# A hybrid two-layer backbone on one core: a weight split ahead of the mLSTM rows, layer 0's last two product blocks together, and keys, values and queries in 512 columns

## The chip, the cores and the metric

The kernel runs on 1 core of one Trainium2 chip. A core has TensorE (PE, matrix products), VectorE (DVE), ScalarE (ACT), GpSimd (POOL) and SyncE (SP, which issues most DMAs). Each engine works through its own instructions in a fixed order and waits at semaphores for the others. The metric is the device time of one execution in microseconds (us).

## The reference, cut to what matters

The inputs are 512 latent tokens `x` and 256 context tokens `ctx`, 1024 wide, a conditioning vector, and the weights of two layers. All arithmetic is float32. Only the latent stream is the output.

```python
for l in range(2):
    h_lat, h_ctx = modulate(x, ...), modulate(ctx, ...)      # RMSNorm * (1+scale) + shift
    if l == 0:  y_ctx, y_lat = mixer_ab(...)   # h @ w_in -> HGRN2 heads and mLSTM heads -> @ w_out
    else:       y_ctx, y_lat = mixer_c(...)    # attention, 8 query heads, 2 key/value heads
    x = x + g1 * rmsnorm(y_lat, norm_g[l, 1])
    x = x + g2 * rmsnorm(swiglu(modulate(x, ...), ffn_w_in[l], ffn_w_out[l]), norm_g[l, 3])
    if l == 0: the same two lines for ctx

def swiglu(h, w_in, w_out):                    # d_ff = 2816
    g, u = split(h @ w_in); return (silu(g) * u) @ w_out

def mixer_c(h_ctx, h_lat, w_qkv, qk_g, w_out, ang, need_ctx):    # the last layer needs no y_ctx
    q, k, v = split(h @ w_qkv, [1024, 1280])   # 8, 2 and 2 heads of 128
    q, k = rmsnorm(q, qk_g[0]), rmsnorm(k, qk_g[1])              # over the 128 of a head
    latent tokens: q, k = rope2d(q, ang), rope2d(k, ang)
    return softmax(q @ k_all.T) @ v_all @ w_out

mLSTM gates, per head and direction (running over tokens, reset at the start):
    m_t = max(logf_t + m_{t-1}, i_t);  b_t = sum of logf in the chunk;  weights exp(i - b), exp(-m), ...
```

## The kernel before, in words

**Products.** Every float32 operand of a product is split into a high part (rounded on ACT) and a low part (the difference, on DVE), and a product is three matmuls: high by high, high by low, low by high. `wsplit` loads a weight piece of 128 x 1024 (`raw`) by a DMA on SP's queue, makes `wh` on ACT (L128) and `wl` on DVE (L129), and keeps both instructions in `self.split`. `w_main`, `w_ext` and `w_more` do this from three rings of buffers. `proj_t` (L163) makes columns of features, `proj_n` (L181) rows of tokens: for a pair of token tiles and 256 weight columns, 2 tiles x 8 depths x 3 = 48 matmuls. Results stand in PSUM: two buffers `psa` of 1024 columns, three `psb` of 512, one `psc`.

**Order.** A scheduler puts the program's operations on each engine's queue; its order is not that of the source everywhere, but follows it. `self.after(n, fn)` queues a piece of work until `deferred()` has been called n times: by this the vector work behind a product, and the transposes of its result, are put behind later products. `behind(cx, insts)` holds what is written in its block back until the given instructions have been issued.

**Layer 0.** The HGRN2 heads are scanned one after another; while a head is scanned, a generator (`dense`) issues the next products. For the last head this is `mlstm_first`: the gates, the row operations over all tokens (`mlstm_rows`, scans on DVE, L924 to L955), the values (`v_group`, L181), then the query and key chunks `mlstm_qk(0)` and `(2)`, each with a weight of 128 columns (2560 and 2816) through L163. The scan of the last HGRN2 head uses L718 (transposes), L728 (state updates into `psb`), L733 and L735 (DVE, which read that `psb`) and L745 (scores into `psb`).

**Layer 0's second FFN product** (`ffn0_out`, L1528) goes over two halves of three token tiles and 11 blocks of 256 features. In each block each of the three tiles gets 12 matmuls of 512 columns; after the last block each tile is finished by `end`: residual and norm (`residual`: ACT L194 sums squares, DVE L188 adds the epsilon, POOL L189 takes the power, DVE L1135 and L1142), a second norm (L194, L188, L189, L1153), and, for a pair of tiles, transposes on PE (L388), scale and shift on ACT (L395) and the split into `hh`, `hl` on DVE (L402, L403), which are the moving operand of layer 1. The third tile of a half is summed in two `psb` and copied out first (L1492).

**Layer 1's projections** (`mixer1`): keys of a pair of tiles, values of that pair, three pairs; then queries of two heads at a time (256 columns) for the two latent pairs. A unit's result is squared (L1657) and copied (L1660) on ACT, summed (L1662), scaled (L1665 or L1669), rotated (L1683, L1686, L1687) on DVE, transposed on PE (L1695) and split (L1698, L1699). Values are split at L1722, L1723. Scores are L1773, the row maximum L1776, the exponential L1779, the transposes of probabilities L1789, the sums with values L1802. The output projection is `mixer1_out` (L1226), then comes the FFN of layer 1, whose first products (L163, `early`) run for two runs of 256 tokens each. The last token tile is finished by half rows (L1238 to L1246).

The constants that the change touches are:

```python
L1D = 2
L1E = 3
A1 = (3, 3, 2)
```

## Time and profile before

| | us |
|---|---|
| median of 3 runs (1667.42 to 1667.67) | 1667.49 |
| profiled execution | 1672.43 |
| its span | 1670.7 |
| PE busy in the span | 1616.4 (97%) |
| DVE busy | 1094.4 (66%) |
| ACT busy | 677.9 (41%) |
| POOL busy | 140.4 (8%) |

The mean granted clock of TensorE over the span was 0.989. Times in the profile are microseconds from the span's start. A timeline row gives start, duration, engine, line of the kernel, operation, output <- inputs and, in brackets, how long the engine stood idle before and for whom. Matmuls are pipelined, so their durations overlap. Line numbers are those of the kernel before; in the changed kernel they are 2 to some 25 higher.

### The profile page before, as it was taken

How to read it: one execution, taken by the hardware profiler on the slowest of the kernel's cores; microseconds unless marked ns; L12 is line 12 of the kernel's file. 1: busy time of each engine (PE TensorE's matmuls, PEld its weight loads, DVE VectorE, ACT ScalarE, POOL GpSimd, SP SyncE). 2: the span in 40 equal slices, each digit the busy share in tenths (PEclk: the TensorE clock that was granted, in tenths of full speed). 3: DMA queues.
4: the chain of work that ended last, by engine and by line, in shares of the span. 5: the costliest groups of instructions: out<-in, count | busy, mean ns of one | idle time of the engine just before them, and what ended most of it. 6: DMA issues, size and time to landing. Idle time of an engine off the chain costs nothing. (4 is left out here: it accounts for less than half of the span.)

```text
span 1670.7 us, 25343 instructions
## 1 busy us (share of the span) xinstructions
PE 1616.4 (97%) x10257; PEld 1427.5 (85%) x10257; DVE 1094.4 (66%) x1718; ACT 677.9 (41%) x1026; POOL 140.4 (8%) x222
## 2 busy tenths in 40 slices
PE   7999989999999999999999999899999999999997
PEld 4888878889888999999988888898898888888885
DVE  5797996655446989898856674677765533343444
ACT  4565653435335333333334453435663432222221
POOL 2000010001000001000010010212220000000001
PEclk9999999999999999999999999899999999999998
DMA  9333102223624554454439875230004623333321
GB/s 331 94 115 89 27 14 64 77 90 94 209 79 125 178 156 134 142 181 130 157 137 321 313 263 170 96 106 21 26 30 139 204 83 101 101 101 101 91 74 50
DMA packets 172289, 209.38 MB, mean 125 GB/s; under 512 B 7952, under 2 KB 143212, under 8 KB 172172
## 3 DMA queue, kind: packets, MB, share of 16 engines
q1 hardware_dynamic: 167676, 194.85, 36.7%
q0 software_dynamic: 4208, 12.59, 2.1%
q8 instruction: 80, 1.31, 0.3%
q14 instruction: 37, 0.30, 0.1%
q10 hardware_dynamic: 288, 0.33, 0.1%
HBM read 189.62 MB, written 18.12 MB: 124 GB/s over the span
## 5 line engine op out<-in xcount | busy, mean ns | idle before, releaser
L129 DVE TENSOR_TENSOR wl<-raw,wh 128x1024 fp32r<-128x1024 f32 x166 | 201.9, 1222 | 220.1 <-ACT wh L128 219.1
L128 ACT CAST wh<-raw 128x1024 fp32r<-128x1024 f32 x166 | 174.0, 1053 | 395.9 <-PE psa L163 122.7
L181 PE MATMUL psa<-wh,hh 128*128 128x256 f32 x608 | 175.3, 288 | 0.8 <-DVE qn L1669 0.7
L181 PE MATMUL psa<-wl,hh 128*128 128x256 f32 x608 | 173.7, 286 | 0.0
L181 PE MATMUL psa<-wh,hl 128*128 128x256 f32 x608 | 173.4, 285 | 0.0
L163 PE MATMUL psa<-h1h,wh 128*128 128x512 f32 (+1 forms) x384 | 142.8, 372 | 0.0
L163 PE MATMUL psa<-h1l,wh 128*128 128x512 f32 (+1 forms) x384 | 142.7, 372 | 0.0
L163 PE MATMUL psa<-h1h,wl 128*128 128x512 f32 (+1 forms) x384 | 142.6, 371 | 0.0
L181 PEld LDWEIGHTS psa<-wh,hh 128*128 128x128 f32 x608 | 117.5, 193 | 5.0 <-issue 3.5
L181 PEld LDWEIGHTS psa<-wl,hh 128*128 128x128 f32 x608 | 117.6, 193 | 0.8 <-issue 0.8
L181 PEld LDWEIGHTS psa<-wh,hl 128*128 128x128 f32 x608 | 117.6, 193 | 0.3 <-issue 0.2
L189 POOL TENSOR_TENSOR r<-e,mhalf 128x1 f32<-128x1 f32 (+2 forms) x61 | 51.0, 837 | 673.4 <-DVE e L188 673.3
L1528 PE MATMUL psa<-wh,gh 128*128 128x512 f32 x352 | 100.9, 396 | 2.6 <-ACT gh L1476 2.0
L1340 PE MATMUL psa<-hh,wX 128*128 128x384 f32 x320 | 89.8, 339 | 1.3 <-DVE ed L1360 1.3
L163 PEld LDWEIGHTS psa<-h1l,wh 128*128 128x128 f32 x384 | 72.3, 188 | 12.5
L163 PEld LDWEIGHTS psa<-h1h,wh 128*128 128x128 f32 x384 | 72.3, 188 | 12.4
L163 PEld LDWEIGHTS psa<-h1h,wl 128*128 128x128 f32 x384 | 72.3, 188 | 12.4
L1528 PEld LDWEIGHTS psa<-wh,gh 128*128 128x128 f32 x352 | 65.8, 190 | 18.8 <-ACT gh L1476 3.2
L311 DVE SCALAR_TENSOR_TENSOR oall<-oall,sil 128x1024 f32<-128x1024 f32 x50 | 62.3, 1278 | 2.4 <-DMA oall<-in_ada_w_dram 2.3
L1340 PEld LDWEIGHTS psa<-hh,wX 128*128 128x128 f32 x320 | 58.5, 188 | 4.4 <-DVE ed L1360 2.0
L163 PE MATMUL psa<-hh,wl 128*128 128x256 f32 x208 | 54.9, 343 | 5.8 <-DVE wl L129 5.8
L163 PE MATMUL psa<-hh,wh 128*128 128x256 f32 x208 | 55.4, 344 | 0.0
(454 smaller groups left out, 3848.7 us busy)
## 6 DMA issues: line engine op xcount, KB each, us to landing
raw<-in_ffn_w_in_dram SPq DMA_DIRECT2D x68, 512.0 KB, 3.8
raw<-in_ffn_w_out_dram SPq DMA_DIRECT2D x66, 512.0 KB, 4.2
adaw<-in_ada_w_dram SPq DMA_DIRECT2D x46, 512.0 KB, 4.5
oall<-in_ada_w_dram SPq DMA_DIRECT2D x34, 512.0 KB, 4.5
raw<-in_ab_w_in_dram SPq DMA_DIRECT2D x32, 512.0 KB, 4.1
rawu<-in_ffn_w_in_dram SPq DMA_DIRECT2D x20, 512.0 KB, 4.5
gd<-g POOLq DMA_DIRECT2D x22, 384.0 KB, 3.8
gr<-gd SPq DMA_DIRECT2D x22, 384.0 KB, 4.6
```

The costliest lines, as they stand in the source:

```text
L128: self.split = [nc.scalar.copy(hi, raw).ins, nc.vector.tensor_tensor(lo, raw, hi.bitcast(F32), ALU.subtract).ins]
L129: nc.vector.tensor_tensor(lo, raw, hi.bitcast(F32), ALU.subtract).ins]
L163: mm(ps[:, o:o + n], st[:, k, :], mv[:, k, t0:t0 + n], start=first, stop=last)
L181: mm(o, a[:, k, t0:t0 + P], b[:, k % 4, :], start=k == 0 and j == 0, stop=k == KD - 1 and j == 2)
L189: self.powered = nc.gpsimd.tensor_tensor(r, e, self.mhalf[:, :n], ALU.pow).ins
L311: nc.vector.scalar_tensor_tensor(av, wv, self.sil[:, k, v:v + 1], av, ALU.mult, ALU.add)
L1340: mm(dst, s[:, k, :], v[:, k, :], start=first and k == 0 and j == 0, stop=k == 3 and j == 2, skip_group_check=True)
L1528: mm(ys[ti][hf], st, mv[:, 0, hf * 512:(hf + 1) * 512], start=b == 0 and j == 0 and st is ah and mi == 0, stop=b == NF // 2 - 1 and j == 1 ...
```

## The change

Five edits:

1. `mlstm_first` issues the first step of the values and loads and splits the weight of columns 2560 first; the row operations are held behind the DVE half of that split (`self.split[1:]`).
2. In `ffn0_out` the last two blocks of a half are worked as one group: each token tile gets the four weight chunks, 24 matmuls of 512 columns, in one go, and is finished after them. `A1` goes from (3, 3, 2) to (3, 2, 2).
3. In `mixer1` keys and values are one product of 512 columns (`key_values`), and so are the queries of heads 0 to 3; heads 4, 5 and 6, 7 keep 256 columns. The weight pieces are then 2 depths x 512 columns, four of them. The ring of extra buffers grows from 4 to 6; the transposes of keys and of heads 0 to 3 are put off by one `deferred()`, those of heads 6, 7 by four (`L1E`).
4. The first products of layer 1's FFN move into `ffn_early`, whose first half runs ahead of the last deferred work of `mixer1_out`.
5. For the last tile, the epsilon's addition (`eps_added`, line L188) is what the deferred work of the tile before is held behind, in place of the addition of the two partial sums.

The core of the diff:

```diff
-L1E = 3
+L1E = 4
-A1 = (3, 3, 2)
+A1 = (3, 2, 2)
...
     def proj_n(self, ws, hT, pair):
...
+        m, n = ws[0][0].shape[1:]
         for t in range(2):
-            o = ps[:, t * 512:t * 512 + 256]
+            o = ps[:, t * 512:t * 512 + n]
...
-        self.mlstm_rows()
-            run(v_group(3072, 0, self.vb, 129))
+            values = v_group(3072, 0, self.vb, 129)
+            next(values)
+            ws = self.chunk_w(2560)
+            with ExitStack() as cx:
+                self.behind(cx, self.split[1:])
+                self.mlstm_rows()
+            run(values)
             yield
-            for b in (0, 2):
-                self.qk[b] = self.mlstm_qk(b)
+            self.qk[0] = self.mlstm_qk(0, ws)
+            self.qk[2] = self.mlstm_qk(2)
...
-        self.added = [nc.vector.tensor_tensor(ms[:, 0:1], ms[:, 0:1], ms[:, 1:2], ALU.add).ins]
+        nc.vector.tensor_tensor(ms[:, 0:1], ms[:, 0:1], ms[:, 1:2], ALU.add)
         r = self.rstd(ms[:, 0:1], 1)
+        self.added = [self.eps_added]
...
+            group = range(n, n + 2 if b == NF // 2 - 2 else n + 1)
+            for m in group:
+                if m + 2 < len(blocks):
+                    prep(m + 2)
+                self.steps(bg, 1 + half)
...
+            ops = [(*ready[m][0:2], ready[m][2], j) for m in group for j in range(2)]
...
-                if b == NF // 2 - 1:
+                if len(ops) == 4:
                     end(3 * half + ti, tiles[ti])
...
+    def ffn_early(self, l, hT):
+
+        early = {c: list(self.halves(l, c)) for c in (0, 1)}
+        for d in range(2):
+            for c in early:
+                for w, ps in early[c]:
+                    self.proj_t(ps, *w, *hT, segs=((256 * d, 256 * d, 256),))
+            self.deferred()
+            yield
+        self.early = {c: [ps for _, ps in x] for c, x in early.items()}
...
+            def unit(c0, pair, later=1):
                 ps = self.proj_n(ws[c0], hT, pair)
...
                 self.deferred()
+                for n in range(0, ps.shape[2], 256):
+                    queries(c0 + n, ps[:, :, n:n + 256], pair, later)
+
+            def key_values(pair):
+                ps = self.proj_n(ws[1024], hT, pair)
+                self.deferred()
+                kn = self.qk_norm(ps[:, :, 0:256], tp, False)
...
+                self.after(1, lambda: self.to_t(kn, kh, kl, 0, pair * 256))
...
+                for pair in range(3):
+                    key_values(pair)
...
+                ws[0] = self.natural_w(w2, 0, (self.w_ext,) * 3 + (self.w_main,), 512)
+                for pair in (1, 2):
+                    unit(0, pair)
+                ws[512] = self.natural_w(w2, 512)
+                for pair in (1, 2):
+                    unit(512, pair, L1D)
+            ws[768] = self.natural_w(w2, 768, (self.w_more, self.w_main))
+            rest = [1, 2]
+            self.attend(qh, ql, kh, kl, vh, vl, lambda: unit(768, rest.pop(0), L1E) if rest else None)
...
-        self.deferred(2)
+        self.deferred()
...
+                early = self.ffn_early(1, (hh, hl))
+                next(early)
+            for _ in early:
+                pass
```

What the schedule makes of it, at three places. In the rows below a name's last number counts the buffers of a program; the two programs number them apart.

DVE at the mLSTM rows, before: `wl_2933` is the low part of the weight of columns 2560, `wl_3008` that of 2816; L955 is the last of the row operations, L733 and L735 belong to the HGRN2 scan.

```order
L951 COPY bt_2670<-z_2514 32x6
L952 COPY bt_2670<-z_2514 32x6
L955 TENSOR_TENSOR cf_2680<-ig_2512,z_2514 64x768
L129 TENSOR_TENSOR wl_2933<-raw_2930,wh_2932 128x1024
L129 TENSOR_TENSOR wl_3008<-raw_3005,wh_3007 128x1024
L974 TENSOR_TENSOR m_2650<-z_2514,m_2650 64x768
L733 COPY st_2863<-psb_2864 128x128
```

The same place now, first ahead of the rows (L934 is the first scan) and then behind them (L738 and L740 are the old L733 and L735):

```order
L692 TENSOR_TENSOR suf_2629<-dec_2621 128x6
L129 TENSOR_TENSOR wl_2720<-raw_2717,wh_2719 128x1024
L693 TENSOR_TENSOR pre_2628<-pre_2628,dec_2621 128x6
L694 TENSOR_TENSOR suf_2629<-suf_2629,dec_2621 128x6
L934 SCALAR_TENSOR_TENSOR m_2723<-lf_2516,ig_2512 32x768
```

```order
L961 COPY bt_2743<-z_2514 32x6
L962 COPY bt_2743<-z_2514 32x6
L965 TENSOR_TENSOR cf_2753<-ig_2512,z_2514 64x768
L129 TENSOR_TENSOR wl_3008<-raw_3005,wh_3007 128x1024
L738 COPY st_2869<-psb_2870 128x128
```

One of the two splits moved ahead of the scans, the other did not; L974 moved behind the scan's steps.

DVE at the end of layer 0, before: `x_1500_10002` is the last token tile, L1153 writes its normalised rows, which PE transposes; the L402/L403 are those of the pair of tiles before.

```order
L1135 TENSOR_TENSOR x_1500_10002<-x_1500_10002,G_9266 128x1024
L1662 TENSOR_REDUCE msq_10115<-qsq_10113 128x4
L402 CAST hh_8545<-mod_10129 128x2x256
L188 TENSOR_SCALAR e_10117<-msq_10115 128x4
L403 TENSOR_TENSOR hl_8546<-mod_10129,hh_8545 128x2x256
L402 CAST hh_8545<-mod_10139 128x2x256
L402 CAST hh_8545<-mod_10149 128x2x256
L403 TENSOR_TENSOR hl_8546<-mod_10139,hh_8545 128x2x256
L403 TENSOR_TENSOR hl_8546<-mod_10149,hh_8545 128x2x256
L402 CAST hh_8545<-mod_10159 128x2x256
L403 TENSOR_TENSOR hl_8546<-mod_10159,hh_8545 128x2x256
L1142 SCALAR_TENSOR_TENSOR x_1500_10002<-x_1500_10002,r_10009,res_10000 128x1024
```

And now (L404, L405 are the old L402, L403; L1145, L1152 and L1163 the old L1135, L1142 and L1153; `x_1508_10042` is the last tile):

```order
L404 CAST hh_8545<-mod_10018 128x2x256
L405 TENSOR_TENSOR hl_8546<-mod_10018,hh_8545 128x2x256
L404 CAST hh_8545<-mod_10028 128x2x256
L405 TENSOR_TENSOR hl_8546<-mod_10028,hh_8545 128x2x256
L190 TENSOR_SCALAR e_10048<-ms_10046 128x1
L1145 TENSOR_TENSOR x_1508_10042<-x_1508_10042,G_9266 128x1024
L1152 SCALAR_TENSOR_TENSOR x_1508_10042<-x_1508_10042,r_10049,res_10040 128x1024
L190 TENSOR_SCALAR e_10106<-ms_10104 128x1
L1163 TENSOR_SCALAR res_10040<-x_1508_10042,r_10107 128x1024
```

The four pairs of L402/L403 stand ahead of the whole chain of the last tile instead of in its middle; on PE they belong to transposes that now follow the last L1528 at once.

DVE behind the second unit of 512 query columns, now (`ql` is the low part of transposed queries, whose `psb` PE has just written; `qn_10562` and `qn_10580` are the two halves of the unit, `msq_10675` belongs to the unit of 256 that follows; L1679, L1682, L1700, L1703, L1704 and L1716 are the old L1662, L1665, L1683, L1686, L1687 and L1699):

```order
L129 TENSOR_TENSOR wl_10766<-raw_10763,wh_10765 128x1024
L1716 TENSOR_TENSOR ql<-psb_10546,qh 128x2x256
L1716 TENSOR_TENSOR ql<-psb_10553,qh 128x2x256
L1679 TENSOR_REDUCE msq_10564<-qsq_10560 128x4
L190 TENSOR_SCALAR e_10566<-msq_10564 128x4
L1682 TENSOR_TENSOR qn_10562<-qn_10562,r_10567 128x512
L1700 TENSOR_TENSOR rot_10571<-qn_10562,sg_10220 128x4x32 x4
L1679 TENSOR_REDUCE msq_10582<-qsq_10578 128x4
L1703 TENSOR_TENSOR qn_10562<-qn_10562,cg_10219 128x512
L190 TENSOR_SCALAR e_10584<-msq_10582 128x4
L1704 TENSOR_TENSOR qn_10562<-qn_10562,rot_10571 128x512
```

PE's transposes of these two halves (L1712, the old L1695) stand 10 and 39 products of 256 columns into the unit after the next, with one whole narrow unit ahead of them; before, each such transpose had one or two whole narrow units ahead of it:

```order
L183 MATMUL psa_10689<-wh_10598,hh_8545 128x256
L1712 MATMUL psb_10657<-ident,qn_10562 128x128 x4
L183 MATMUL psa_10689<-wl_10599,hh_8545 128x256
L183 MATMUL psa_10689<-wh_10598,hl_8546 128x256
L183 MATMUL psa_10689<-wh_10604,hh_8545 128x256
```

The number of matmuls falls by 240 (those of L181 from 1824 to 1584); the numbers of DVE, ACT, POOL and DMA instructions stay.

More of the change, by code (lines that the diff above doesn't have):

```diff
@@ L1509, in ffn0_out @@
         prep(1)
-        for n, (half, b) in enumerate(blocks):
+        n = 0
+        while n < len(blocks):
+            half, b = blocks[n]
             if b == 0:
@@ L1514, in ffn0_out @@
                 tiles.append(ys[2])
-            if n + 2 < len(blocks):
-                prep(n + 2)
-            self.steps(bg, 1 + half)
+            group = range(n, n + 2 if b == NF // 2 - 2 else n + 1)
[3 more added lines that the diff above has]
+                self.steps(bg, 1 + half)
             if half and b < 4:
                 self.deferred()
-            gh, gl, w = ready.pop(n)
+            ops = [(*ready[m][0:2], ready[m][2], j) for m in group for j in range(2)]
+            n = group[-1] + 1
             for ti in range(3):
-                for j in range(2):
+                for q, (gh, gl, w, j) in enumerate(ops):
                     s = slice(ti * P, (ti + 1) * P)
@@ L1533, in ffn0_out, with halves @@
                     pieces.pop(0)()
+    def halves(self, l, c):
+        both = self.psa()
+        for n in range(2):
+            w = (self.w_more if (c, n) == (1, 1) else self.w_main)(self.cols(self.i["ffn_w_in"][l], n * DFF + c * P), KD, P)
+            yield w, both[:, n * 512:(n + 1) * 512]
+    def ffn_early(self, l, hT):
[7 more added lines that the diff above has]
+        self.early = {c: [ps for _, ps in x] for c, x in early.items()}
     def ffn(self, l, hT, tiles, pool, emit, yacc, bg=iter(())):
@@ L1550, in ffn @@
             c += nb
-        def half_w(c, n):
-            return (self.w_more if (c, n) == (1, 1) else self.w_main)(self.cols(win, n * DFF + c * P), KD, P)
-        def halves(c):
-            both = self.psa() if lat_only else None
-            for n in range(2):
-                yield ahead.pop((c, n), None) or half_w(c, n), both[:, n * 512:(n + 1) * 512] if lat_only else self.psa()
-        ahead = {(c, n): half_w(c, n) for c in range(2) for n in range(2)}
         def products(bi, gt, wo):
@@ L1592, in ffn @@
         G = None
[L1594 to L1601 removed]
+        early = self.early
         for bi, blk in enumerate(blocks):
@@ L1609, in ffn @@
                     pg = []
-                    for n, (w, ps) in enumerate(halves(c)):
+                    for w, ps in self.halves(l, c):
                         self.proj_t(ps, *w, *hT, segs=segs)
@@ L1853, in mixer1_out @@
                                                              c0=(i // 2 - 1) * 256))
-        self.deferred(2)
+        self.deferred()
     def run(self):
```

76 lines of the change are left out of this document (27 added, 49 removed).

## The prediction

> **What bounds the kernel now.** I read the page first, then the waits of TensorE (PE), then the timeline around each long wait.
>
> ```profile
> PE 1616.4 (97%) x10257; PEld 1427.5 (85%) x10257; DVE 1094.4 (66%) x1718; ACT 677.9 (41%) x1026; POOL 140.4 (8%) x222
> ...
> PE psa L163 <- DVE wl L129: 5.8, 1, 5.8
> PE psb L388 <- DVE res L1153: 4.1, 3, 2.7
> PE psb L1695 <- DVE qn L1687: 2.4, 1, 2.4
> PE psa L1773 <- ACT pr L1779: 2.3, 2, 1.9
> PE psa L1528 <- ACT gh L1476: 2.0, 1, 2.0
> ```
>
> PE is busy for 97% of the span, so a change can win in two ways only: fewer or shorter PE steps, and shorter stops of PE. The second group of rows (us in total, times, longest) names the stops in the places that are edited. What a matmul costs is not its listed duration, since matmuls overlap; it is the distance between two starts:
>
> ```profile
> 1300.29 0.28 PE L163 MATMUL psa<-h1h,wl 128*128 128x256 f32 x1
> 1300.41 0.28 PE L163 MATMUL psa<-h1h,wh 128*128 128x256 f32 x1
> ...
> 1274.75 0.62 PE L1226 MATMUL psa<-wh,ql 128*128 128x512 f32 x2
> 1275.20 0.62 PE L1226 MATMUL psa<-wh,qh 128*128 128x512 f32 x2
> ```
>
> 256 columns take 0.120 us (48 of L181 take 5.76), 512 columns 0.226 (two in 0.453). A stop costs more than itself when the granted clock drops after it:
>
> ```profile
> 1057.00:1080.00 23.00, 18.77 (x123) 17.64 (x122) 17.74 (x37) 12.17 (x25) 4.95 (x5) 0.78 0.29 98
> ...
> 1146.80:1150.20 3.40, 1.61 (x9) 0.96 (x7) 3.40 (x10) 1.95 (x5) 0.91 (x1) 1.00 0.00 0
> 1150.20:1153.60 3.40, 2.93 (x11) 2.74 (x12) 2.53 (x6) 0.59 (x3) 0.91 (x1) 0.50 0.00 0
> ```
>
> The columns after the length are busy times of PE, weight loads, VectorE (DVE), ScalarE (ACT), GpSimd (POOL), then the clock. After 3.4 us in which PE worked only 1.61, the next 3.4 us ran at 0.50, worth up to 1.7 us of work.
>
> The sum below is made against the profiled execution, 1672.43 us (span 1670.7, 1.7 around it), which is 4.9 above the median of runs, 1667.49; differences are carried over to the median unchanged.
>
> **The change, part by part**
>
> *1. Split ahead of the mLSTM rows.*
>
> ```profile
> 249.04 0.95 DVE L955 TENSOR_TENSOR cf<-ig,z 64x768 f32<-64x768 f32 x1
> 249.91 2.35 DVE L129 TENSOR_TENSOR wl<-raw,wh 128x1024 fp32r<-128x1024 f32 x2
> 254.15 0.29 DVE L733 COPY st<-psb 128x128 f32<-128x128 f32 x1 [1.02 <-PE psb L728]
> 255.51 0.35 DVE L735 SCALAR_TENSOR_TENSOR st<-st,dt,psb 128x128 f32<-128x128 f32 x1
> ...
> 256.84 0.30 PE L745 MATMUL psb<-qe,sp 128*32 128x64 f32 x7
> ```
>
> PE now stands 5.8 us for the first of two splits, which DVE does only after the row scans. In the new order that split runs before the scans, so this wait goes. But the next thing is late then: the second group of L745 writes a PSUM buffer whose last reader is L735, and L735 still stands behind the scans and the other split. The rows now end one split (1.15) later, at 251.1; then the other split to 252.2, L733 to 252.5, two L735 (0.35 each, one start 0.38 after the other) to about 253.3, PE at 253.4 instead of 256.84: 3.4 earlier. Four of L163 that stood ahead are still to be done (0.7), and the half clock after the stop now falls on the work behind it (about 0.7 more). Gain **2.0**; bounds 1.0 (the stop keeps its length) and 3.4.
>
> *2. Last two blocks of layer 0's second product together, and the normalising of its last tile.*
>
> ```profile
> 1051.04 0.62 PE L1528 MATMUL psb<-wh,gh 128*128 128x512 f32 x2
> 1057.25 1.47 PE L388 MATMUL psb<-ident,res 128*128 128x128 f32 x12
> 1068.93 3.19 PE L388 MATMUL psb<-ident,res 128*128 128x128 f32 x13 [2.75 <-DVE res L1153]
> ...
> 1059.03 1.22 DVE L1135 TENSOR_TENSOR x<-x,G 128x1024 f32<-128x1024 f32 x1
> 1064.76 1.28 DVE L1142 SCALAR_TENSOR_TENSOR x<-x,r,res 128x1024 f32<-128x1024 f32 x1
> 1068.12 0.75 DVE L1153 TENSOR_SCALAR res<-x,r 128x1024 f32<-128x1024 f32 x1 [0.72 <-POOL r L189]
> ```
>
> The product ends at T = 1051.5. The chain of its last tile (L1135, L1142, L1153) is done only 17.4 after T, because four pairs of L402/L403 stand ahead of L1142 on DVE, and PE stops 2.75. With two stops of 0.74 beside it, and about 4 for the clock (0.78 over 23 us is 10.1 us at half; some 8 of them with work), the place loses 8.5. In the new order each tile finishes 24 products of 512 (5.4 us) apart, so the transposes L388 of tiles 2 and 3 start at T. Chain from T, with the durations that the same instructions have in this stretch: the eight L395 and two L1492 on ACT to 5.85, its sum of squares to 6.9; L1135 to 8.35; POOL's power to 8.7; L1142 to 10.1; squares to 11.3; POOL and L1153 to 12.9, PE can go at **13.0**. Cover on PE from T: 16 L388 (0.1 apart, 1.6), 48 key-and-value products of 512 (10.9), and 0.65 of short waits for L395 and L1492: **13.15**. So the stop just goes; gain 8.5 less 1.0 left over = **7.5**; if the chain is one or two us late, that comes back one for one (bounds 4 and 8.5). The four DMA weight loads of the pair are issued one block earlier; they land while 72 products run. They cost nothing, or, with that cover gone, one more wait like the 2.0 that L1528 has for an input now.
>
> *3. 512 columns.* Keys with values (three pairs of tiles) and four heads' queries (two pairs): 480 steps of 256 become 240 of 512. 240 x (0.240 - 0.2265) = **3.2**; bounds 2.9 and 3.6 from the rounding of the rows.
>
> By the Trainium skill, "TensorE: Matmul & The Clock Gate", section "Back-to-back issue gap", the gap between matmuls is N/2.4 + 2.5 ns, so a pair would save only 2.5 ns and all 240 would save 0.6 us. The rows above stand 13 ns over N/2.4 at both widths; the measurement decides.
>
> *4. The queries' way back.* This is what the wide products cost. A group of 512 gives two chains (normalise, rotate, transpose L1695), and in the new order both are wanted after only one narrow product.
>
> ```profile
> 1117.02 0.60 PE L1695 MATMUL psb<-ident,qn 128*128 128x128 f32 x4
> 1123.21 0.60 PE L1695 MATMUL psb<-ident,qn 128*128 128x128 f32 x4
> ...
> 1123.29 1.05 ACT L128 CAST wh<-raw 128x1024 fp32r<-128x1024 f32 x1 [4.45 <-PE psa L181]
> 1124.37 1.23 DVE L129 TENSOR_TENSOR wl<-raw,wh 128x1024 fp32r<-128x1024 f32 x1 [0.59 <-ACT wh L128]
> 1124.73 0.58 ACT L1660 COPY qn<-psa 128x512 f32<-128x512 f32 x1
> 1125.51 0.68 DVE L1662 TENSOR_REDUCE msq<-qsq 128x4 f32<-128x512 f32 x1
> 1126.11 0.68 DVE L1699 TENSOR_TENSOR ql<-psb,qh 128x512 fp32r<-128x512 f32 x1
> 1128.05 0.69 DVE L1665 TENSOR_TENSOR qn<-qn,r 128x512 f32<-128x512 f32 x1 [1.19 <-POOL r L189]
> 1130.43 0.69 DVE L1687 TENSOR_TENSOR qn<-qn,rot 128x512 f32<-128x512 f32 x1
> ```
>
> A unit of 256 with its transposes takes 6.19 (so the four transposes 0.42). A chain ends 7.9 after its unit (1123.21 to 1131.1), and today it has two units, 12 us. Now, counted from the end E of the second wide query unit: PE has two transposes (0.84), one narrow unit (5.76), ten steps (1.2): it asks at E+7.8. The chain holds one more L1699 and one more L1662 (0.60 each by their starts): E+9.1. A stop of 1.3. The second chain ends 5 us after it (its L1665 waits for POOL, then L1683, a foreign L1662, L1686, a foreign L1699, L1687), PE has 0.42 + 29 x 0.12 = 3.9: a stop of 1.0. The unit after it needs a PSUM buffer that ACT has copied out (L1660) 2.1 after its unit's end, and PE has only six L1773 (three of 256 and three of 512 columns, 1.04): a stop of 1.0. The next chain is 1.25 late by the same sums. Together a loss of **4.5**. Below, 0 (the scheduler's order leaves enough slack after all); above, 4.5 and three half-clock windows, 9.6.
>
> By the Trainium skill, the same page, section "HAM oscillation — how this bites in real kernels", PE's idle gaps hurt the clock from about 3.4 us on; none of these four stops would then. The trace draws the line lower: 1.79 idle us in one window already brought 0.50.
>
> *5. First scores.*
>
> ```profile
> 1148.65 0.93 DVE L1776 TENSOR_REDUCE mx<-psa 128x1 f32<-128x768 f32 x1
> ```
>
> The maximum for the second scores moves ahead of a query's L1665 on DVE (today, the row above, it stands behind it, L1699 and L1683, and L1773 waits 1.9): the scores start 1.4 to 1.9 earlier, and the transpose after them (1.7) is waited for instead; gain **1.2** (0 to 2.5). With L1E = 4 the last L1695, waited for 2.4 today, is asked for one step later, but the next L1773 waits for the exponential 2 us at the same place: **0.4** (0 to 2).
>
> *6. Layer 1's first products between the two halves.*
>
> ```profile
> 1302.90 1.20 PE L388 MATMUL psb<-ident,res 128*128 128x128 f32 x9 [0.89 <-DVE res L1153]
> ```
>
> Today 54 steps of 0.12 stand ahead of this transpose, then 96, so the 0.89 goes; behind it L163 waits some 0.4 for the first L403. Gain **0.5** (0 to 1).
>
> *7. The last tile.*
>
> ```profile
> 1661.70 1.28 DVE L1142 SCALAR_TENSOR_TENSOR yacc<-yg,r,res 128x1024 f32<-128x1024 f32 x1 [0.37 <-POOL r L189]
> 1663.77 1.41 DVE L1246 SCALAR_TENSOR_TENSOR yacc<-yg,r,res 128x512 f32<-128x512 f32 x2 [0.73 <-POOL r L189]
> ```
>
> L188 and POOL's power go ahead of the L1142 that ends at 1663.0, and end under it; L1246 starts there instead of at 1663.77: **0.8** (0.5 to 0.9).
>
> Sum: 2.0 + 7.5 + 3.2 - 4.5 + 1.2 + 0.4 + 0.5 + 0.8 = 11.1 us. Profiled 1661.3, median **1656.4**.
>
> **The rivals**
>
> *The queries' chains are covered.* For it: DVE still waited for POOL in each chain (the 1.19 above), and two chains can fill each other's waits. Against: the orders count 7.8 against 9.1. Without the 4.5: 1651.9.
>
> *The last tile of layer 0 is still late.* Cover and chain differ by 0.15 us, over some 30 instructions. A stop of 2.4 brings the half clock, 1.7: 1656.4 + 4.1 = 1660.5, up to 1664.
>
> *The whole first stop goes.* 5.8 and its half clock, 8 instead of 2: 1650.4. Against it stands L735's place.
>
> *Slower: DVE sets the pace of the second layer's projections.* Only two wide PSUM buffers turn over, each must be read by DVE before the unit after next, and DVE's row from T to the second query unit has hardly a gap. If each of nine units stopped 2.1 us, that ate the gains without part 4 (15.6) and 3.3 more; a stop of 2.4 with 1.7 of half clock at six units is 24.6: 1676.5. Against: the same DVE work fits today, and the sums leave 0.7 to 2 us before each wide unit's transposes.
>
> *Listed durations count.* L181's rows of 288 ns against 396 for L1528's 512 columns would make the wide products worth 240 x 0.18 = 43 us.
>
> ```profile
> L181 PE MATMUL psa<-wh,hh 128*128 128x256 f32 x608 | 175.3, 288 | 0.8 <-DVE qn L1669 0.7
> L1528 PE MATMUL psa<-wh,gh 128*128 128x512 f32 x352 | 100.9, 396 | 2.6 <-ACT gh L1476 2.0 <-DVE x L1135 0.4 <-DVE gh L1477 0.2
> ```
>
> Then 1613; the starts 0.12 apart speak against it.
>
> **How the numbers follow.** Forecast (1653 to 1660) 0.50; queries covered (1652) 0.22; last tile late (1660 to 1665) 0.18; whole first stop gone (1650) 0.05; DVE sets the pace (1676) 0.04; durations 0.01. The range 1650.0 to 1663.5 leaves out the last three but half of the 0.05, and the upper end of the late tile, some 0.15 in all. About 0.2%, 3.3 us, can be told from no change; above 1664.2 lie the worst late tiles and small failures of several terms (0.06 between 1664.2 and 1670.8), slower is the DVE case: 0.90, 0.06, 0.04.
>
> **What would show it.** Right: no wait of L163 for L129, but one of 5 to 6 us of L745 for L735; no wait over 1 us of L388 for L1153 at the layer's change and a clock of 1.00 over the 20 us after it; L181 with 240 fewer steps and 0.226 apart; waits of L1695 for L1687 of 1 us or more, twice or thrice, some 20 us ahead of the first probabilities. Wrong: those waits missing or with a clock of 0.50 behind them; a wait for L1153 of over 2 us; or new waits for weights (L128, L129) in the wide units, which I take as covered.

## The result and the profile after

The changed kernel took 1658.81 us (median of 4 runs, 1658.64 to 1660.79), the kernel before 1667.58 beside it (1667.42 to 1667.76): ratio 0.995, 95% interval 0.9933 to 0.9967. In the later comparisons the kernel before spread more (1667.4 to 1674.3); there the change, timed again, took 1659.13 (1658.36 to 1662.08) against 1669.95: ratio 0.9938 (0.9922 to 0.9954). The gain is 9 to 11 us; 11.1 were forecast, and a time of 1656.4 (1650.0 to 1663.5).

The page of the kernel after, first its busy time, then the waits of PE (total, times, longest, in us); the last two rows are of the kernel before:

```profile
PE 1607.6 (97%) x10017; PEld 1409.2 (85%) x10017; DVE 1094.7 (66%) x1718; ACT 677.5 (41%) x1026; POOL 139.1 (8%) x222
```

```profile
...
PE psb L750 <- DVE st L740: 6.2, 5, 3.1
PE psb L1712 <- DVE qn L1704: 4.0, 3, 2.3
PE psb L733 <- ACT kn L724: 3.1, 2, 2.0
...
PE psa L183 <- ACT qn L1677: 0.9, 1, 0.9
PE psb L1712 <- DVE e L190: 0.9, 1, 0.9
```

```profile
PE psb L745 <- DVE st L735: 3.2, 4, 1.3
...
PE psb L728 <- ACT kn L719: 0.9, 1, 0.9
```

PE has 240 instructions fewer, 10257 to 10017, the pairs of 256 that became 512. Of the waits that stood at the top before, L163 for L129 (5.8) is gone, and L388 (now L390) for L1153 went from 4.1 to 0.5. Three have grown: L750 (L745 before) for L740 (L735) from 3.2 to 6.2, L1712 (L1695) for L1704 (L1687) from 2.4 to 4.0, and L733 (L728) for ACT from 0.9 to 3.1.

The profiled executions differ by 13.7 us in span (1670.7 to 1656.9), more than the medians. Laid out by stages, from one PE mark to the next:

| place (step of the forecast) | before | after | gain | forecast |
|---|---|---|---|---|
| last HGRN2 head, from its last transposes (L718) to L1046 of the mLSTM scan (1) | 37.87 | 37.53 | 0.3 | 2.0 |
| from the end of layer 0's second product to the output projection (2 to 5) | 192.59 | 184.80 | 7.8 | 7.8 |
| output projection to layer 1's FFN (6) | 51.44 | 51.20 | 0.2 | 0.5 |
| last product to the end (7) | 11.63 | 10.10 | 1.5 | 0.8 |
| all places without a term in the forecast | 1377.13 | 1373.27 | 3.9 | 0 |

The last row is hardly the change's. About 1.3 of it is one stretch at half clock, 873.7 to 877.1 in the profile before (the first half of layer 0's second product, in which it falls, took 97.26 there and 95.97 after); a second profile of the changed kernel has such a stretch at 871.1. The rest is spread over the span. Without this row 9.9 us are left, inside what the timed runs show.

That the second row equals its forecast is luck. The same stretch, not edited, took 190.84 in the profile of edit 1 alone and 188.64 in that of edits 4 and 5 alone, since the half clock falls differently in each. The part of it up to the last step of keys and values is steadier: 47.92 before (three windows of half clock), 47.28 (two) and 45.11 (none) in those two, and 37.2 in all nine profiles that hold edit 2 and wide keys and values.

The third row ends ahead of the stop that edit 4 aims at. Taken to the end of layer 1's first products it is 77.32 and 77.12, the same 0.2.

**Layer 0's end.** The transposes of its last tiles, in the kernel after, and a window over the place (PE, weight loads, DVE, ACT, POOL, then the clock, as in the prediction):

```profile
1060.23 1.47 PE L390 MATMUL psb<-ident,res 128*128 128x128 f32 x12
...
1061.94 0.66 PE L390 MATMUL psb<-ident,res 128*128 128x128 f32 x4
```

```profile
1046.00:1066.00 20.00, 20.00 (x104) 16.21 (x103) 14.45 (x25) 13.92 (x27) 3.50 (x4) 1.00 0.50 165
```

No wait stands in brackets, PE is busy for all of 20 us, and the clock is 1.00. Before, the same stretch had 2.75 for L1153 and a clock of 0.78. DVE ended L1163 (the old L1153) at 1059.74, 0.5 us before PE came to the transposes at 1060.23; the forecast had 0.15 between them (13.0 and 13.15).

**The queries.** PE's rows in the kernel after, with the idle time in brackets:

```profile
1116.26 0.66 PE L1712 MATMUL psb<-ident,qn 128*128 128x128 f32 x4 [1.07 <-DVE qn L1704]
...
1121.27 0.63 PE L1712 MATMUL psb<-ident,qn 128*128 128x128 f32 x4 [0.89 <-DVE e L190]
...
1124.96 0.39 PE L183 MATMUL psa<-wh,hh 128*128 128x256 f32 x1 [0.93 <-ACT qn L1677]
...
1128.40 0.66 PE L1712 MATMUL psb<-ident,qn 128*128 128x128 f32 x4 [0.56 <-DVE qn L1704]
...
1142.30 0.92 PE L1712 MATMUL psb<-ident,qn 128*128 128x128 f32 x4 [2.34 <-DVE qn L1704]
```

The first four are the four stops that the forecast summed: 1.07, 0.89, 0.93 and 0.56 in brackets. By the distances between starts, by which the forecast counted, they are 1.23, 1.05, 1.09 and 0.72, against 1.3, 1.0, 1.0 and 1.25. The last one it did not have.

**The mLSTM rows.** PE's two stops in the last HGRN2 head, and DVE's row between them:

```profile
246.41 1.38 PE L733 MATMUL psb<-v,kn 128*128 128x128 f32 x10 [1.96 <-ACT kn L724]
...
252.59 0.44 PE L750 MATMUL psb<-qe,sp 128*32 128x64 f32 x8 [3.05 <-DVE st L740]
```

```profile
235.26 1.22 DVE L129 TENSOR_TENSOR wl<-raw,wh 128x1024 fp32r<-128x1024 f32 x1
...
236.55 1.74 DVE L934 TENSOR_TENSOR_SCAN m<-lf,ig 32x768 f32<-32x768 f32 x1
...
238.28 0.94 DVE L705 TENSOR_TENSOR q<-qe,suf 128x768 f32<-128x768 f32 x1
239.15 0.94 DVE L707 TENSOR_TENSOR b<-ke,pre 128x768 f32<-128x768 f32 x1
...
249.36 0.95 DVE L965 TENSOR_TENSOR cf<-ig,z 64x768 f32<-64x768 f32 x1
250.24 1.21 DVE L129 TENSOR_TENSOR wl<-raw,wh 128x1024 fp32r<-128x1024 f32 x1
251.48 0.29 DVE L738 COPY st<-psb 128x128 f32<-128x128 f32 x1
...
251.81 0.35 DVE L740 SCALAR_TENSOR_TENSOR st<-st,dt,psb 128x128 f32<-128x128 f32 x1
```

The end of the chain is as forecast: the rows end at 250.3, the other split at 251.4, the updates L740 at 251.8 and later, PE goes at 252.59, where 253.4 was forecast in a trace that ran 0.6 later. But DVE now has a split and the first scan (L129 and L934, together 3 us) ahead of L705 and L707, from which ACT's `kn` for L733 comes, and PE stops 1.96 for it. That stop is new at this place. It costs nothing by itself: DVE goes from the rows to L740 without a pause, so without the first stop PE would stand that much longer at L750.

### The profile page after: what moved, and what is told of

It reads as the page before. It is cut to its first block, busy times and chain, and to the rows that moved or that the text cites. A ratio compares the mean times of both kernels' runs of the same rounds, so it can differ in the third digit from the quotient of the medians.

```text
span 1656.9 us, 24856 instructions
## 1 busy us (share of the span) xinstructions
PE 1607.6 (97%) x10017; PEld 1409.2 (85%) x10017; DVE 1094.7 (66%) x1718; ACT 677.5 (41%) x1026; POOL 139.1 (8%) x222
## 3 DMA queue, kind: packets, MB, share of 16 engines
q8 instruction: 78, 1.28, 0.3%
## 4 chain that ended last, share of the span: by engine, by line
PE 63%; DVE 3%; POOL 1%; issue 1%; ACT 0%; DMA 0%; DVEq 0%; POOLq 0%; ACTq 0%
PE psa L163 15%; PE psa L1351 13%; PE psa L1236 9%; PE psa L1545 7%; PE psb L1351 5%; PE psa L183 4%; PE psb L1545 4%; PE psc L1823 2%; PE psa L1794 2%; PE psb L1810 1%; PE psa L1310 1%; PE psb L390 1%; PE psb L1310 1%; DVE wl L129 0%; PE psc L327 0%
## 5 line engine op out<-in xcount | busy, mean ns | idle before, releaser
L129 DVE TENSOR_TENSOR wl<-raw,wh 128x1024 fp32r<-128x1024 f32 x166 | 201.5, 1222 | 218.0 <-ACT wh L128 215.2
L183 PE MATMUL psa<-wh,hh 128*128 128x256 f32 (+1 forms) x528 | 160.0, 303 | 0.9 <-ACT qn L1677 0.9
L183 PE MATMUL psa<-wl,hh 128*128 128x256 f32 (+1 forms) x528 | 158.7, 301 | 0.0
L183 PE MATMUL psa<-wh,hl 128*128 128x256 f32 (+1 forms) x528 | 158.4, 300 | 0.0
L163 PE MATMUL psa<-h1l,wh 128*128 128x512 f32 (+1 forms) x384 | 142.8, 372 | 0.2 <-DVE h1l L405 0.2
L163 PE MATMUL psa<-h1h,wl 128*128 128x512 f32 (+1 forms) x384 | 142.6, 371 | 0.0
L163 PE MATMUL psa<-h1h,wh 128*128 128x512 f32 (+1 forms) x384 | 142.5, 372 | 0.0
L183 PEld LDWEIGHTS psa<-wh,hh 128*128 128x128 f32 x528 | 100.7, 191 | 7.7 <-issue 3.5
L183 PEld LDWEIGHTS psa<-wl,hh 128*128 128x128 f32 x528 | 100.8, 191 | 3.7 <-DVE wl L129 0.4
L183 PEld LDWEIGHTS psa<-wh,hl 128*128 128x128 f32 x528 | 100.7, 191 | 3.3 <-issue 0.2
L163 PEld LDWEIGHTS psa<-h1l,wh 128*128 128x128 f32 x384 | 72.3, 188 | 12.8 <-DVE h1l L405 0.4
L163 PEld LDWEIGHTS psa<-h1h,wl 128*128 128x128 f32 x384 | 72.3, 188 | 12.6
L163 PEld LDWEIGHTS psa<-h1h,wh 128*128 128x128 f32 x384 | 72.2, 188 | 12.6
L163 PE MATMUL psa<-hh,wh 128*128 128x256 f32 x208 | 56.2, 348 | 0.0
L163 PE MATMUL psa<-hl,wh 128*128 128x256 f32 x208 | 55.8, 347 | 0.0
```

Source lines behind the costliest of these rows:

```text
L129: nc.vector.tensor_tensor(lo, raw, hi.bitcast(F32), ALU.subtract).ins]
L163: mm(ps[:, o:o + n], st[:, k, :], mv[:, k, t0:t0 + n], start=first, stop=last)
L183: mm(o, a[:, k, t0:t0 + P], b[:, k % m, :], start=k == 0 and j == 0, stop=k == KD - 1 and j == 2)
```

## The experiments

All ratios are to runs of the kernel before in the same comparison, with a 95% interval; gains in us are worked out from the ratio.

**Each edit alone.** Edit 1 alone (rows behind a split), on the kernel before:

```diff
-            self.mlstm_rows()
-            run(v_group(3072, 0, self.vb, 129))
+            values = v_group(3072, 0, self.vb, 129)
+            next(values)
+            ws = self.chunk_w(2560)
+            with ExitStack() as cx:
+                self.behind(cx, self.split[1:])
+                self.mlstm_rows()
+            run(values)
```

> The kernel before with edit 1 alone (the split of columns 2560 ahead of the mLSTM rows). Theory, from the profile after: PE's wait for the split only turns into a wait of L745 for L735 (3.1 us there) and of L728 for the cast kn on ScalarE (2.0), and the place gains 0.3 us: 1667.2, not to be told from no change. Rival, the sum of the prediction: 2.0 us, 1665.6.

Measured: 0.9989 (0.9976 to 1.0003), 1669.66 us; 1.8 us, and no change is not excluded. Its stage took 35.03 where the whole change, with the same order of work, took 37.53 in one profile and 36.34 in another. Four variants below keep this order too; theirs took 34.96, 35.03, 37.16 and 37.51. In the four profiles with the old order it took 37.47 to 37.87. The second stop ends equally long after the stage's transposes in all seven; what differs is where the half clock falls. Windows of edit 1 alone, then of the whole change:

```profile
245.80:249.20 3.40, 1.44 (x12) 1.13 (x10) 3.29 (x9) 3.38 (x7) 0.00 (x0) 1.00 0.00 0
249.20:252.60 3.40, 3.39 (x55) 2.50 (x53) 3.23 (x13) 0.14 (x1) 0.00 (x0) 0.50 0.00 0
252.60:256.00 3.40, 1.75 (x53) 1.63 (x54) 3.27 (x14) 0.00 (x0) 0.00 (x0) 1.00 0.48 152
```

```profile
247.80:251.20 3.40, 1.74 (x52) 1.33 (x52) 3.25 (x12) 0.00 (x0) 0.00 (x0) 1.00 0.00 0
251.20:254.60 3.40, 2.01 (x49) 1.88 (x50) 3.15 (x14) 0.00 (x0) 0.00 (x0) 0.56 0.49 158
254.60:258.50 3.90, 3.90 (x14) 3.29 (x13) 3.51 (x4) 0.34 (x1) 0.00 (x0) 0.51 0.02 6
```

Alone, the half clock lies between the two stops, on work that would have waited at the second stop anyway. In the other execution it lies over the second stop and behind it, where PE has no slack, and lasts for two windows.

Edit 2 alone (last two blocks together):

```diff
-A1 = (3, 3, 2)
+A1 = (3, 2, 2)
...
+            group = range(n, n + 2 if b == NF // 2 - 2 else n + 1)
+            for m in group:
...
+            ops = [(*ready[m][0:2], ready[m][2], j) for m in group for j in range(2)]
```

> The kernel before with edit 2 alone (last two blocks of layer 0's second product together, and its A1). Theory: the stop of L388 for L1153 and the half clock behind it belong to this edit alone; it brings 6 to 8 us: about 1660.5. Rival: the long product of 512 columns is the cover that hides the last tile's chain, so that with keys and values apart (5.8 us each) part of the stop stays: 2 to 4 us, about 1664.

Measured: 0.9964 (0.9953 to 0.9976), 1665.53 us, a gain of 6.0. From the end of layer 0's product to the output projection it took 186.35, 6.2 less than before; up to the last step of keys and values 41.24, where 45.11 to 47.92 were needed without an edit. Two waits are left there, for the last tile's scale and shift and for the read-out of a key unit:

```profile
1064.37 0.66 PE L388 MATMUL psb<-ident,res 128*128 128x128 f32 x4 [0.24 <-ACT mod L395]
...
1066.22 0.39 PE L181 MATMUL psa<-wh,hh 128*128 128x256 f32 x1 [1.20 <-DVE qn L1676]
```

Edit 3 alone (512 columns, L1E = 4):

```diff
+            def key_values(pair):
+                ps = self.proj_n(ws[1024], hT, pair)
...
+                ws[0] = self.natural_w(w2, 0, (self.w_ext,) * 3 + (self.w_main,), 512)
+                for pair in (1, 2):
+                    unit(0, pair)
```

> The kernel before with edit 3 alone (keys with values and four heads' queries in 512 columns, L1E = 4). Theory: 3.2 us of steps are won and about 4 us of stops of L1695 and L181 behind the second wide query unit are paid; the stop at the change of layers stays: 1667 to 1669, no gain. Rival: the wide products win their 3.2 us and the stops seen in the profile after belong to the earlier arrival that edit 2 brings: 1664.4.

Measured: 0.9982 (0.997 to 0.9993), 1668.54 us, a gain of 3.0. The same stretch took 186.4 in its profile, 6.2 less too, and up to the last step of keys and values 39.02. Its waits hold what the change has at the queries (first row), and at the layer's change a smaller wait than before (second row, PE's timeline):

```profile
PE psb L1697 <- DVE qn L1689: 4.0, 3, 2.3
```

```profile
1066.03 1.42 PE L390 MATMUL psb<-ident,res 128*128 128x128 f32 x11 [1.20 <-DVE res L1155]
```

So wide products lose their 3.5 us (in brackets) at the queries and still gain, since a wide key-and-value product is also a longer cover for the last tile: its wait fell from 2.75 to 1.20, without a half clock behind it in this execution. Up to the last step of keys and values, against the 45.11 of a profile without half clock there, edit 2 alone gains 3.9, edit 3 alone 6.1, and both together 7.9, less than their sum, because both remove the same stop.

Edits 4 and 5 alone (`ffn_early`, `eps_added`):

```diff
-        self.deferred(2)
+        self.deferred()
...
+                early = self.ffn_early(1, (hh, hl))
+                next(early)
...
+        self.added = [self.eps_added]
```

> The kernel before with edits 4 and 5 alone (layer 1's first products between the two halves, and the last tile's epsilon). Theory, the prediction's sum: 0.5 + 0.8 = 1.3 us, 1666.3; the two profiles read 0.2 + 1.5 = 1.7. Rival: DMA of the output ends the span and hides edit 5: 0.3, 1667.2.

Measured: 0.998 (0.997 to 0.999), 1666.62 us, a gain of 3.3, more than forecast. The tail is 1.53 shorter (11.63 to 10.10, the same in every profile with the edit). The stop that edit 4 aims at was 0.89 in the profile before, but 1.57, 1.53 and 2.01 in the profiles of edits 1, 2 and 3 alone; with edit 4 it is 0.30, and 0.22 behind it. Nothing is edited at the layer's change, and its stop is all there; but see the window over it:

```profile
1067.61 1.20 PE L390 MATMUL psb<-ident,res 128*128 128x128 f32 x9 [2.75 <-DVE res L1155]
```

```profile
1060.00:1080.00 20.00, 15.54 (x128) 14.83 (x128) 16.24 (x34) 10.01 (x19) 3.16 (x4) 1.00 0.27 86
```

With 4.5 us idle in 20 the clock stayed at 1.00, where the profile of the kernel before shows three windows of half clock after the same stop. So the same stop brings the half clock in some executions and not in others; the last section shows on what it depends. The four parts' gains add to 0.85%, with an uncertainty of some 0.2% by their intervals.

**The change again**, beside variants.

> The changed kernel itself, timed on the chip of the four kernels with one part each. Those took 0.11, 0.36, 0.18 and 0.20% off, 0.85% in all. Theory: edits 2 and 3 hide the same stop (L388 for L1153 at the change of layers; with edit 3 alone it fell from 2.9 to 1.4 us and lost its half clock), so their gains overlap by 3 to 4 us: 0.60 to 0.70%. Rival: the parts add up: 0.85%.

Measured: 0.9938 (0.9922 to 0.9954), 1659.13 us: 0.62%, as the theory has it, though the two uncertainties together do not quite exclude 0.85%. The overlap itself is seen in the profiles above, 7.9 against 3.9 and 6.1.

**Queries of heads 0 to 3 in 256 columns**, keys and values wide:

```diff
-                ws[0] = self.natural_w(w2, 0, (self.w_ext,) * 3 + (self.w_main,), 512)
-                for pair in (1, 2):
-                    unit(0, pair)
...
+                for g in range(3):
+                    ws[g * 256] = self.natural_w(w2, g * 256, (self.w_ext, self.w_main))
+                    for pair in (1, 2):
+                        unit(g * 256, pair, L1D)
```

> The changed kernel with keys and values in 512 columns, but heads 0 to 3's queries in two units of 256 with their transposes two units later, as before. Theory: the wide queries win 96 steps of 13.5 ns = 1.3 us and pay stops of 1.2, 1.05, 1.1 and 0.7 us: without them the kernel is 2.8 us (0.17%) faster than the change. Rival: the stops come from keys and values arriving late, and stay: 1.3 us slower than the change.

Measured: 0.9962 (0.9949 to 0.9975), 1663.95 us, by the medians slower than the change by some 4.8, where 2.8 faster was expected. The stops at the queries are nearly gone, 0.9 in all, but a new one stands where the first narrow unit follows the last wide one (waits, then PE's row):

```profile
PE psa L183 <- DVE vl L1751: 3.8, 1, 3.8
...
PE psb L1712 <- DVE qn L1704: 0.9, 2, 0.7
```

```profile
1096.23 0.48 PE L183 MATMUL psa<-wh,hh 128*128 128x256 f32 x1 [3.85 <-DVE vl L1751]
```

Each unit fills one of two `psa`, so a unit must last until DVE has read the unit before it. A wide unit lasts 11.0 us, a narrow one 5.8; DVE reads the values (L1751) at 1095.5 to 1096.2, behind two splits and the key's norm, and PE starts at 1096.23. In brackets, the change pays for the wide queries with 3.5 us and would lose 3.85 at once without them.

**The second wide unit's transposes one unit later:**

```diff
-                    unit(0, pair)
+                    unit(0, pair, pair)
```

> The changed kernel with the transposes of the second wide query unit put off by one more unit (later = 2 for pair 2), nothing else. Theory: those two transposes were asked 7.8 us behind their unit and their rows come at 9.1 and 14.1; asked 13 us behind it the first two stops (1.2 and 1.05) go, and the copy wait behind them may: 2.3 to 3.3 us faster than the change. Rival: VectorE sets the pace, and the wait moves on to the next transposes or scores: no gain.

Measured: 0.9932 (0.9916 to 0.9949), 1658.5 us, not to be told from the change. PE's rows:

```profile
1121.14 0.63 PE L1712 MATMUL psb<-ident,qn 128*128 128x128 f32 x4 [0.61 <-DVE qn L1704]
...
1126.51 0.66 PE L1712 MATMUL psb<-ident,qn 128*128 128x128 f32 x4 [2.13 <-DVE qn L1704]
...
1134.51 0.66 PE L1712 MATMUL psb<-ident,qn 128*128 128x128 f32 x4 [0.32 <-DVE qn L1704]
```

The first two stops became 0.61, and the next grew to 2.13. Counted from the end of layer 0's second product, DVE finished that chain 2.2 us earlier than in the change, but PE came for it 3.8 earlier.

**One multiplication less in each query's chain.** The output lacks the cosine factor of the queries' rotation:

```diff
-        nc.vector.tensor_tensor(q4, q4, cg[:, ti:ti + 2, :].unsqueeze(2).broadcast_to([P, 2, 2, P]), ALU.mult)
+        if w:
+            nc.vector.tensor_tensor(q4, q4, cg[:, ti:ti + 2, :].unsqueeze(2).broadcast_to([P, 2, 2, P]), ALU.mult)
```

> The changed kernel without the multiplication of the queries by the cosine table (L1686, 0.69 us for each of eight halves of queries); the queries are wrong by that factor. Theory (VectorE's pace, and the length of each chain): the stops of L1695 of 1.23 and 1.05 become 0.6 and below 0.5, and of the 7.5 us of stops from there to the first probabilities 2 to 4 go. Rival: the transposes wait for the split ahead of the chains or for PSUM: the stops stay within 0.3 us.

Measured: one run, 1659.66 us. PE's rows:

```profile
1119.33 0.66 PE L1713 MATMUL psb<-ident,qn 128*128 128x128 f32 x4 [1.07 <-DVE qn L1705]
...
1123.51 0.63 PE L1713 MATMUL psb<-ident,qn 128*128 128x128 f32 x4 [1.02 <-DVE qn L1705]
...
1129.23 0.66 PE L1713 MATMUL psb<-ident,qn 128*128 128x128 f32 x4 [1.29 <-DVE qn L1705]
...
1136.37 0.66 PE L1713 MATMUL psb<-ident,qn 128*128 128x128 f32 x4 [0.74 <-DVE qn L1705]
```

The first chain is 0.7 shorter, counted from the end of its wide unit (8.2 instead of 8.9), and the stop is as long as before, since the scheduler put the transposes six products earlier on PE's queue (52 narrow products ahead of them instead of 58) and the next ones another eight earlier. So the run does not tell a late chain from a DVE without slack. It shows something else: the place of the transposes on PE's queue is no given, and in both kernels the scheduler asks for the first chain 1.07 us before the chip has it done. The stretch from layer 0's second product to the output projection took 181.80, where the change took 184.80 and 184.64; up to 1.7 of these 3.0 is a stretch of half clock that both profiles of the change have there and this run has not.

**The rows behind the head's last state update:**

```diff
-            with ExitStack() as cx:
-                self.behind(cx, self.split[1:])
-                self.mlstm_rows()
             run(values)
             yield
+            with ExitStack() as cx:
+                self.behind(cx, [self.st_last])
+                self.mlstm_rows()
```

> The changed kernel with the mLSTM row operations held behind the last state update L735 of the HGRN2 scan (written ahead of the chunk of columns 2560), not ahead of it. Theory: L745's wait for L735 (3.1 us) and its half clock (2.5 us in the profile of the change) go, the wait for the cast kn (2.0) may shrink: 3 to 6 us faster than the change. Rival: the rows then end some 12 us later and PE waits for them at the mLSTM scan instead: no gain, or slower.

Measured: 0.9954 (0.9939 to 0.9969), 1661.95 us, by the medians 2.8 slower than the change (the intervals overlap), where 3 to 6 faster was expected. The two stops of 1.96 and 3.05 are gone, and two others came, because what the rows feed is late:

```profile
PE psb L786 <- DVE ats L774: 4.4, 1, 4.4
...
PE psb L1119 <- DVE et L1112: 2.2, 1, 2.2
```

**The rows in two parts**, the scans for the maximum where the change has them, the rest behind the last state update (`mlstm_rows` yields between them):

```diff
-                self.mlstm_rows()
+                rows = self.mlstm_rows()
+                next(rows)
             run(values)
             yield
+            with ExitStack() as cx:
+                self.behind(cx, [self.st_last])
+                run(rows)
```

> The changed kernel with the row operations in two pieces: the three scans of the maximum (3.7 us of VectorE) where the change has them, the rest (the twelve scans of sums, the copies, L955: about 8 us) behind the last L735 of the HGRN2 scan. With all of them late, PE had no stop there but waited 4.4 us for the sum ats and 2.2 for et later. Theory: VectorE has 4 us less to do behind the scan, so both late waits fall to about 0.5 and the stops of 2.1 and 3.2 stay away: 4 to 6 us faster than the change. Rival: VectorE's total work between 230 and 270 us is what counts, and what is taken from one stop comes back as another: within 1.5 us of the change.

Measured: 0.9929 (0.9912 to 0.9945), 1658.08 us; by itself not to be told from the change, and less than the 4 to 6 us expected. PE's rows:

```profile
246.61 1.38 PE L733 MATMUL psb<-v,kn 128*128 128x128 f32 x10 [1.53 <-ACT kn L724]
...
270.04 0.49 PE L786 MATMUL psb<-v,ats 128*128 128x128 f32 x2 [2.16 <-DVE ats L774]
```

The stop of 3.05 is gone and half of the 4.4 is left at L786. The stage took 34.44, where seven profiles with the change's order took 35.0 to 37.5.

**The output projection's weights later.** Its first three splits are held behind the fourth block of attention sums, since one of them (1.22 us of L129 on DVE at 1128.87 in the profile after) stands ahead of the chain for which PE waits 2.34 at 1142.30:

```diff
-            w.append((self.w_main if k < 3 else self.w_more if k == 3 else self.w_ext)(src, 1, D))
+            with ExitStack() as cx:
+                self.behind(cx, self.mixed[3:4] if k < 3 else [])
+                w.append((self.w_main if k < 3 else self.w_more if k == 3 else self.w_ext)(src, 1, D))
```

> The changed kernel with the first three weight loads of the attention's output projection (two of their splits, 2.3 us of VectorE, stand among the queries' last chains) held behind the fourth sum with values. Theory: VectorE sets the pace from the second wide query unit to the first probabilities, so 2.3 us less of it shorten the stops there (1.1, 0.7, 0.5, 2.5) by 1.2 to 2.3 us. Rival: the stops are the length of a chain (ScalarE, POOL, VectorE in turn), not VectorE's load: no change.

Measured: 0.9928 (0.9914 to 0.9943), 1658.34 us. PE's rows at the place:

```profile
1135.11 0.61 PE L1794 MATMUL psa<-kh,qh 128*128 128x256 f32 x2 [1.14 <-ACT pr L1800]
...
1139.52 0.63 PE L1712 MATMUL psb<-ident,qn 128*128 128x128 f32 x4 [0.73 <-DVE qn L1704]
...
1140.76 0.39 PE L1823 MATMUL psc<-ptl,vh 128*128 128x256 f32 x1 [0.61 <-DVE ptl L1814]
```

2.34 became 0.73 and 0.61, and a stop of 1.14 ahead of them is where the change has 0.44 and 0.23. From the first scores to the output projection it took 107.60 instead of 109.04, without the half clock that stood behind the stop. The timed gain is smaller than one comparison resolves.

**Both together** (rows in two parts, weights later):

> The changed kernel with both: the rows in two pieces and the three weight loads later. The two places are 800 us apart, so the gains add: theory 5 to 8 us faster than the change (about 0.99 of the kernel before). Rival: neither gains, 0.994 as the change.

Measured: 0.9916 (0.9901 to 0.993), 1655.99 us (1654.89 to 1656.91). Its runs lie below all eight runs of the change (1658.36 to 1662.08), which were timed in other comparisons; the two intervals of the ratio, 0.9901 to 0.993 and 0.9922 to 0.9954, still overlap. By the medians it is the best version: some 3 us under the change, where 5 to 8 were expected, and 14 under the kernel before. In its profile both stages have the length that each part gave alone (34.44 and 107.6), and only one window of 3.4 us ran at half clock between the start and the tail; the change had three in one profile and four in another, the kernel before eight.

## Why the prediction was right, step by step

The time (1658.8 and 1659.1 against 1656.4) and the sign are right, and by the profiles the sum is 9.9 against 11.1. That it comes so near is in part luck: steps 1 and 5 brought 4.4 us less than forecast, and the layer's change, the queries and the tail 2.6 more, while the half clock moves single places by 2 to 3 us between executions of the same code. The steps:

*Split ahead of the rows (2.0).* The mechanism was right. Counted from the head's last transposes, the second group of L750 starts 3.6 us earlier than in the profile before (3.4 forecast), and at the same point in all seven profiles with this order; the four L163 behind it take 0.8. The term that failed is the half clock, booked at "about 0.7 more": it cost 2.5 in one profile of the change, 1.3 in the other, and nothing in three others, where it lay between the two stops. So the gain was 0.3 and 1.5 in the two profiles of the change, 2.8 in that of edit 1 alone and 1.8 timed; the bounds, 1.0 to 3.4, were too narrow below. That L705 and L707 come later was not foreseen either, so the one wait of 5 to 6 us that was named as a sign came as two, 1.96 and 3.05. The rival that the whole first stop goes is refuted by them.

*Last two blocks together (7.5).* Right: the stop just goes, PE is busy for the whole stretch. Up to the last step of keys and values the change gains 10.7 on the profile before, of which three wide units are 1.7. The 9.0 that are left are more than forecast; 2.8 of them are half clock, which a profile with the same stop did not have. The forecast made its sum for both edits together: edit 2 alone keeps waits of 0.24 and 1.20 that the wide units of edit 3 then cover. The rival that the last tile is still late is refuted; the margin was 0.5, not 0.15.

*512 columns (3.2).* 2.9. From its first step to the transposes behind it a wide unit takes 11.0 us in three cases without a stop, two narrow units before took 11.59: 0.58 less for each of five. The starts are 0.227 apart at 512 columns (median) and 0.120 at 256, so the rival that listed durations count is refuted.

*The queries' way back (-4.5).* Mechanism and place right, size 4.1 by the distances between starts. No half clock came with the four stops in either profile of the change, so the upper bound of 9.6 was not reached. The rival that they are covered is refuted. Narrow queries would have been worse for a reason that the prediction did not have: the read-out of a wide unit, 3.85.

*First scores (1.2 and 0.4).* Wrong in sign. The maximum did move ahead, but PE's last transpose of queries then waits 2.34 for L1704, and PE's stops around the first scores add up to 3.7 us by the distances between starts, where they were 2.6: a loss of 1.1. Later nothing was gained. The step named the transpose that would be "waited for instead" only with the 1.7 of the profile before, and not what else had come to stand ahead of that chain on DVE, a weight's split. With the splits of the output projection off that place the chain ended 2.5 us earlier, counted from the end of layer 0's second product, and the 2.34 fell to 0.73 and 0.61. So the splits were a cause; a part of the stop moved to L1794.

*Layer 1's first products (0.5):* 0.2 against the profile before, whose stop of 0.89 was shorter than the 1.5 to 2.0 of three others.

*The last tile (0.8):* 1.5, for another reason. L1246 starts 0.9 earlier, as forecast. But the span ends with a drain instruction on POOL that follows POOL's last power and takes 6.71 us in both profiles, longer than the output needs to land. That power comes 1.5 us earlier, and the end with it.

*DVE sets the pace* did not come true: none of the wide key-and-value units stops. Whether the stops at the queries are DVE's lack of slack or the chain's own length stays open; the run made to tell them apart moved the question as well, since the scheduler re-made the order.

Two sums of the prediction are off, without consequence. The parts of the 8.5 us lost at the layer's change (2.75, twice 0.74, and 4) add to 8.2, and the rival on listed durations, with 43 in place of 3.2, comes to 1616.6, not 1613.

## What to carry to other kernels

When two edits lengthen the cover of the same stop, price them together: at the layer's change they earned 3.9 and 6.1 us alone, and 7.9 together. On two PSUM buffers a wider product needs its neighbours to last as long as its read-out; here a narrow unit of 5.8 us behind a wide one of 11.0 stopped PE for 3.85. Work moved on an off-path engine has two prices, what it delays at its new place and what then comes late from it: with weights' splits among the queries' chains PE waited 2.34 us, where 0.73 and 0.61 were left without them, and the rows moved late brought new waits of 4.4 and 2.2. A half clock behind a stop of 2 to 3 us is better priced as a chance than as a fixed sum; the next section shows why.

## What the hardware showed that was not expected

The same stop is followed by half clock in some executions and not in others. After most of 2.75 us of waiting at the layer's change, the kernel before ran three windows of 3.4 us at 0.50; edits 4 and 5 alone, with the same stop in the same place, ran at 1.00. Between the start and the tail, half clock began at 251.6 and 1142.5 in the profile of the change, and at 253.3, 444.4, 871.1 and 1171.5 in another execution of the same kernel. Each window is worth up to 1.7 us, and the kernel before spread over 7 us (1667.4 to 1674.3). The Trainium skill, "TensorE: Matmul & The Clock Gate", section "What's actually happening", says that the clock is judged over windows of 3413 ns that run on freely from before the kernel starts; the stretches of 3.4 us and their changing places agree with that.

The traces show what decides. In each of the 14 profiles all changes of the clock lie whole multiples of 3.413 us apart, so that a profile can be cut into such windows. Between the start and the tail there are 6540 of them at full clock. 37 hold 1.86 us or more in which PE is idle, and each of these is followed by a window at 0.50. 6483 hold 1.66 or less, and none of these is. Of the 20 between, ten are. So what counts here is whether PE stands idle for about half of one window, not the length of a stop. Two windows of the kernel before, then two of edits 4 and 5 alone, over the stop of 2.75:

```profile
1064.90:1068.30 3.40, 1.28 (x11) 1.05 (x10) 1.46 (x3) 1.15 (x2) 0.55 (x1) 1.00 0.41 155
1068.30:1071.70 3.40, 2.77 (x13) 2.48 (x13) 1.26 (x3) 1.77 (x4) 1.01 (x1) 0.50 0.60 166
```

```profile
1063.20:1066.60 3.40, 1.66 (x15) 1.42 (x13) 1.66 (x3) 1.15 (x2) 0.39 (x1) 1.00 0.32 123
1066.60:1070.00 3.40, 1.86 (x13) 1.39 (x13) 1.42 (x3) 1.75 (x4) 1.17 (x2) 1.00 0.57 153
```

In the first, PE works 1.28 of one window, and the next runs at half clock. In the second the stop is shared by two windows with 1.66 and 1.86 of work, and the clock stays. An edit that only moves a stop by a few us can thus differ by 2 us from one execution to the next (the place of edit 1 took 35.0 to 37.5 us with one order of work), and terms below that cannot be read from one pair of profiles.
